# Low parts of seven output-projection weight blocks: a negated high part plus an accumulating DMA in place of a vector subtraction

## The chip, the cores and the metric

The kernel runs on one core of a Trainium2 chip. The metric is device time in microseconds (us) of one execution; three timed runs of the kernel before gave 924.5, 924.59 and 924.91 us (median 924.59). All positions below are us from the start of the profiled span.

## The reference

One decoder layer on a 1024 x 1024 residual stream in float32: RMS norm, an input projection, two head groups (a pooling mixer and a gated linear recurrence), an output projection, a squared-ReLU MLP, a gated embedding and a final norm. The line that matters here is the output projection:

```python
h = h + jnp.concatenate([y_pool, y_lru], axis=-1) @ w_out[l]
z = rms_norm(h, norm_mlp_g[l])
h = h + jnp.square(jax.nn.relu(z @ w_up[l])) @ w_down[l]
```

`w_out` is 1024 x 1024 float32.

## The kernel before

Every product of float32 matrices is made of three matmuls in the type float32r, which keeps fewer bits than float32. Each operand is split into a high part (`hi`, the value rounded to float32r) and a low part (`lo`, what the rounding lost), and `mm` (L341 to L350) issues for each block of 128 input rows `hi*hi`, then `hi` of the weights with `lo` of the data, then `lo` of the weights with `hi` of the data. All these matmuls carry line L350.

A weight block is 128 partitions x 1024 columns (512 KB). It is fetched by `load_weights` (L191): a DMA issued by SP (L196) into a tile `wo<o>_raw`, then `split` (L174): ScalarE (ACT) copies it to `wo<o>_hi` (L178), and VectorE (DVE) subtracts, `wo<o>_lo = raw - hi` (L179). Tiles `raw`, `hi` and `lo` come from pools with two buffers each, so block o+2 cannot be split before the matmuls have read block o, and its raw tile cannot be loaded before the split of an earlier block has read the raw tile whose place it takes.

The output projection has eight blocks o = 0 to 7. Each gives 8 x 3 x 2 = 48 matmuls (eight row blocks k, three products, two halves of 512 columns) into PSUM tiles `ps_o<o>`. Data are `B[0..7]`, the tiles `y0` to `y23`. Blocks 0 and 1 are interleaved (L683 to L697): k = 0 to 5 of block 0, k = 0 to 5 of block 1, k = 6, 7 of block 0, k = 6, 7 of block 1; blocks 2 to 7 follow one after another. After each block DVE adds the result to the residual stream `h` (L701), ACT squares and scales it for the next norm (L386, L389, L706), and after every second block DVE and ACT prepare operands `a` of the MLP.

Weights are asked for in the order of the list `todo` (L316 on), one block ahead. Behind `wo0` to `wo7` come the MLP weights `wu0_0`, `wu0_1`, and so on, which use the same three pools. For the first MLP pair (`up_step` with m = 0) POOL (GpSimd) makes three sums of the raw tiles (`gp`, L215), which ACT and DVE then split. A scheduler orders the instructions of each engine from the program's dependencies; each engine then runs its own list in order, and an instruction that waits holds up all behind it on that engine.

Of the kernel before, what the change touches and what calls it, by code (L numbers as in the profile page):

```python
# [10 lines left out]
AF = mybir.ActivationFunctionType  # L11
ALU = mybir.AluOpType

P = 128
S = 1024
# [6 lines left out]
URGENT = 200  # L22
# [8 lines left out]
NT = D // P  # L31
# [27 lines left out]
def block_kernel(  # L59
# [16 lines left out]
    nc = tc.nc  # L76
# [69 lines left out]
    def f32(ap):  # L146
        return ap.bitcast(F32)
# [22 lines left out]
    def pin(ins):  # L170
        return tc.keep_in_program_order(ins) if in_order else ins
# [3 lines left out]
    def split(src, hi, lo, g=None, eng=None):  # L175

        if g is None:
            first = pin(nc.scalar.activation(hi, src, AF.Copy))  # L178
            lowest[:] = [pin((eng or nc.vector).tensor_tensor(lo, src, f32(hi), ALU.subtract)).ins]  # L179
        else:  # L180
            first = pin(nc.scalar.activation(hi, src, AF.Identity, scale=g))  # L181
            lowest[:] = [pin(nc.vector.scalar_tensor_tensor(lo, src, g, f32(hi), ALU.mult, ALU.subtract)).ins]  # L182
        return first.ins

    def raw_tile(name):
        return wp.tile([P, S], F32, tag="raw", name=f"{name}_raw")

    def weight_tiles(name):
        return [wp.tile([P, S], F32R, tag=f"w{x}", name=f"{name}_{x}") for x in ("hi", "lo")]

    newest = []  # L191

    def load_weights(src, name, width=S, eng=None, queue=nc.sync, offset=0):
# [4 lines left out]
            newest[:] = [split(raw, hi, lo, eng=eng)]  # L198
        return hi, lo

    def split_weights(name, *srcs):

        hi, lo = weight_tiles(name)
        n = 0
        for src in srcs:
            w = src.shape[-1]
            split(src, hi[:, n : n + w], lo[:, n : n + w])
            n += w
        return [(hi[:, hs], lo[:, hs]) for hs in HALVES]
# [26 lines left out]
    def up_step(m, step):  # L236
        name = f"wu{m}_{step}"
        if m == 0:
            if step == 0:
                load_up(0)  # L240
            a, b, a11, a12, a21, a22 = up_blocks(0)
            s1, s2 = (R[:, hs] for hs in HALVES)
            if step == 0:
                gp(ALU.add, s1, a21, a22)
                gp(ALU.subtract, s2, s1, a11)
                gp(ALU.subtract, a21, a11, a21)
                return split_weights(name, s2, a21)
            if step == 1:
                w = split_weights(name, a22, s1)
                load_up(1)  # L250
                return w
            if step == 2:
                w = split_weights(name, a11, a12)
                up_lower[0, 3] = lowest[0]
                dv(ALU.subtract, a12, a12, s2)
                return w
            return split_weights(name, a12)
# [37 lines left out]
    def down_step(c, kind, q):  # L295
# [22 lines left out]
    todo = [  # L318
        (load_weights, w_lru[k * P : (k + 1) * P, :], f"wl{k}", 3 * P)
        for k in range(1, NT)  # L320
    ]
    todo += [(load_weights, w_in[i], f"wi{i}", S, None, nc.sync, URGENT * (i > 2)) for i in range(9)]
    todo += [(load_weights, w_out[o], f"wo{o}", S, None, nc.sync, URGENT * (o == 0)) for o in range(NT)]
    todo += [(up_step, m, step) for m in range(NPAIR) for step in range(4)]
    todo += [(down_step, c, kind, q) for c, kind in KINDS for q in range(NQ)]
    for g, os in enumerate(FETCH):
# [154 lines left out]
    for k in range(NT):  # L481
# [3 lines left out]
        for hs in halves:  # L485
            nc.sync.dma_start(H[k][:, hs], xT[k * P : (k + 1) * P, hs])  # L486
            if k == hs.start == 0:
                raw = raw_tile("wl0")[:, : 3 * P]
# [659 lines left out]
    for g, hs in enumerate(GROUPS):  # L1148
# [5 lines left out]
        for n, o in enumerate(ORDER[g]):  # L1154
# [18 lines left out]
            if g == 0 and 1 <= n < 5:  # L1173
                raw = wp.tile([P, S], F32, tag="raw", name=f"wg0_{n + 3}_raw")
# [100 lines left out]
```

## Time and profile before

| what | value |
|---|---|
| median of three timed runs | 924.59 us |
| the profiled execution's own time | 924.56 us |
| its span, first to last instruction | 922.8 us |
| outside the span | 1.76 us |
| TensorE (PE) busy | 914.6 us, 99% |
| DVE busy | 760.6 us, 82% |
| ACT busy | 459.1 us, 50% |
| POOL busy | 5.8 us, 1% |
| granted TensorE clock, mean | 0.999 |
| DMA moved | 123.97 MB, 134 GB/s |

Rows of groups read: line, engine, operation, out<-in, count, then durations in ns (min/median/max) and first and last start. Rows of a timeline read: start, duration, engine, line, operation, out<-in, count, and in brackets how long the engine idled before it and what ended that. A matmul of 128x512 is shown with 379 ns, but matmuls are pipelined: one starts about 0.216 us after the other. SP's and POOL's DMA issues are given with the time from issue to landing.

### The profile page before, as it was taken

The numbers are of one execution on the slowest core, as the hardware profiler recorded it, in microseconds if no ns is written. First come the engines' busy times: TensorE is split into PE (matmuls) and PEld (weight loads), VectorE is DVE, ScalarE is ACT, GpSimd is POOL, SyncE is SP. The second block draws the span as 40 slices with busy tenths as digits, with TensorE's granted clock in tenths as the row PEclk, the third lists the DMA queues.
The fourth block names the chain that finished last, engine by engine and source line by source line (L and its number), as shares of the span: only waits on it lengthen the run. The fifth ranks groups of instructions, "written<-read, shape, count | busy, mean of one in ns | idle before, by whom it ended". The sixth has DMA issues, their size and how long they took to land.

```text
span 922.8 us, 11209 instructions
## 1 busy us (share of the span) xinstructions
PE 914.6 (99%) x4357; PEld 798.6 (87%) x4357; DVE 760.6 (82%) x915; ACT 459.1 (50%) x535; POOL 5.8 (1%) x7
## 2 busy tenths in 40 slices
PE   9999999999999999999999999999999999999997
PEld 7888888888888888888888888888888888888896
DVE  6997984669998888888888989979786669885676
ACT  7567892447543343334334654443444347652545
POOL 0000000002000000000000000000000000000000
PEclk9999999999999999999999999999999999999999
DMA  7210143112154345344534989366632341031022
GB/s 267 90 56 27 43 167 108 69 45 69 70 189 164 126 169 198 136 141 171 191 125 148 340 315 345 109 198 205 197 114 92 114 160 45 2 136 46 1 92 92
DMA packets 45044, 123.97 MB, mean 134 GB/s; under 512 B 4160, under 2 KB 6208, under 8 KB 44992
## 3 DMA queue, kind: packets, MB, share of 16 engines
q1 hardware_dynamic: 44848, 123.22, 38.2%
q8 instruction: 34, 0.56, 0.2%
q14 instruction: 18, 0.15, 0.1%
q10 hardware_dynamic: 144, 0.04, 0.0%
HBM read 89.69 MB, written 33.55 MB: 134 GB/s over the span
## 4 chain that ended last, share of the span: by engine, by line
PE 98%; DMA 1%; DVE 0%; SPq 0%; ACT 0%; issue 0%; DVEq 0%
PE ps_P_u L350 31%; PE ps_P_d L350 31%; PE ps_i L350 10%; PE ps_e L350 10%; PE ps_o L350 9%; PE ps_l L350 3%; PE ps_j L350 1%; PE ps_g L564 1%; DMA h<-in_xT 1%; PE ps_p L350 1%; PE n_ps L417 0%; PE n_ps L416 0%; DVE t L1123 0%; SPq L486 0%; DVE a L182 0%; ACT a L181 0%
## 5 line engine op out<-in xcount | busy, mean ns | idle before, releaser
L350 PE MATMUL ps_P_d<-a,wd_P_hi 128*128 128x512 f32 x880 | 261.7, 379 | 0.0
L350 PEld LDWEIGHTS ps_P_d<-a,wd_P_hi 128*128 128x128 f32 x880 | 166.3, 189 | 23.6
L350 PE MATMUL ps_P_d<-a,wd_P_lo 128*128 128x512 f32 x440 | 166.8, 379 | 0.0
L350 PE MATMUL ps_P_u<-a,wu_hi 128*128 128x512 f32 x512 | 152.3, 379 | 0.0
L350 PE MATMUL ps_P_u<-y,wu_hi 128*128 128x512 f32 x384 | 114.2, 379 | 0.0
L350 PEld LDWEIGHTS ps_P_u<-a,wu_hi 128*128 128x128 f32 x512 | 96.8, 189 | 13.8
L350 PE MATMUL ps_P_u<-a,wu_lo 128*128 128x512 f32 x256 | 97.0, 379 | 0.0
L350 PEld LDWEIGHTS ps_P_d<-a,wd_P_lo 128*128 128x128 f32 x440 | 83.2, 189 | 11.8
L350 PEld LDWEIGHTS ps_P_u<-y,wu_hi 128*128 128x128 f32 x384 | 72.6, 189 | 10.3
L740 DVE TENSOR_TENSOR t<-t,ps_P_u 128x512 f32<-128x512 f32 (+1 forms) x80 | 62.6, 782 | 20.4 <-PE ps_P_u L350 20.4
L350 PE MATMUL ps_i<-a,wi_hi 128*128 128x512 f32 x288 | 74.3, 380 | 0.0
L350 PE MATMUL ps_P_u<-y,wu_lo 128*128 128x512 f32 x192 | 72.8, 379 | 0.0
L178 ACT ACTIVATE a<-wd 128x1024 fp32r<-128x1024 f32 x56 | 59.0, 1055 | 22.2 <-DMA wd<-act 13.8
L179 DVE TENSOR_TENSOR a<-wd,a 128x1024 fp32r<-128x1024 f32 x56 | 67.2, 1220 | 1.2 <-ACT a L178 0.8
L350 PE MATMUL ps_o<-y,wo_hi 128*128 128x512 f32 x256 | 65.7, 379 | 0.0
L350 PEld LDWEIGHTS ps_i<-a,wi_hi 128*128 128x128 f32 x288 | 54.1, 189 | 8.9 <-issue 1.0
L178 ACT ACTIVATE wu_hi<-wu 128x1024 fp32r<-128x1024 f32 x24 | 25.4, 1059 | 69.8 <-PE ps_P_u L350 44.1
L178 ACT ACTIVATE wu_hi<-wu_raw 128x1024 fp32r<-128x1024 f32 (+1 forms) x26 | 25.3, 976 | 66.3 <-PE ps_P_u L350 41.3
L350 PEld LDWEIGHTS ps_o<-y,wo_hi 128*128 128x128 f32 x256 | 48.4, 189 | 6.8
L350 PEld LDWEIGHTS ps_P_u<-a,wu_lo 128*128 128x128 f32 x256 | 48.4, 189 | 6.8
L178 ACT ACTIVATE wd_P_hi<-wd 128x1024 fp32r<-128x1024 f32 x24 | 25.3, 1055 | 46.4 <-PE ps_P_d L350 46.4
L389 ACT ACTIVATE t<-h 128x512 f32<-128x512 f32 (+2 forms) x44 | 32.0, 732 | 29.0 <-DVE h L1041 21.0
(236 smaller groups left out, 1507.6 us busy)
## 6 DMA issues: line engine op xcount, KB each, us to landing
wd<-act SPq DMA_DIRECT2D x56, 512.0 KB, 5.8
act<-t SPq DMA_DIRECT2D x32, 512.0 KB, 4.4
wu_raw<-in_w_up SPq DMA_DIRECT2D x16, 512.0 KB, 3.3
wu<-in_w_up SPq DMA_DIRECT2D x16, 512.0 KB, 4.0
act<-wu SPq DMA_DIRECT2D x16, 512.0 KB, 4.7
wd<-in_w_down SPq DMA_DIRECT2D x16, 512.0 KB, 6.7
h<-in_xT SPq DMA_DIRECT2D x14, 512.0 KB, 4.4
wg_raw<-in_w_gate SPq DMA_DIRECT2D x10, 512.0 KB, 3.2
```

What stands on the lines that cost most here:

```text
L178: first = pin(nc.scalar.activation(hi, src, AF.Copy))
L179: lowest[:] = [pin((eng or nc.vector).tensor_tensor(lo, src, f32(hi), ALU.subtract)).ins]
L350: ins = nc.tensor.matmul(ps, w, turns(z[:, hs]), start=first and z is zhi and w is whi, stop=last and w is wlo, skip_group_check=more,)
L389: pin(nc.scalar.activation(sq, t[:, hs], AF.Square))
L564: nc.tensor.matmul(x, w[r, o * P : (o + 1) * P], turns(z[r, at : at + HALF]), start=n == 0, stop=n == 2)
L740: (eng or nc.vector).tensor_tensor(to, to if y is None else y, x, ALU.add)
```

## The change

For blocks 1 to 7 the low part is made without DVE. ACT writes the high part as before, then ACT writes `-hi` into the low tile, and a DMA issued by POOL adds the raw weights to the low tile in memory (`accum_op=ALU.add`), so that the tile ends as `raw - hi`. The source of that DMA is the array in DRAM for odd blocks, and the raw tile on chip for even blocks. Block 0 is split as before. `newest` keeps its meaning; `lowest` is not set by the new function.

```diff
+    def load_added(src, name, far):
+        raw = raw_tile(name)
+        hi, lo = weight_tiles(name)
+        nc.sync.dma_start(raw, src)
+        first = pin(nc.scalar.activation(hi, raw, AF.Copy))
+        pin(nc.scalar.activation(lo, f32(hi), AF.Copy, scale=-1.0))
+        nc.gpsimd.dma_start(lo, src if far else raw, accum_op=ALU.add)
+        newest[:] = [first.ins]
+        return hi, lo
...
-    todo += [(load_weights, w_out[o], f"wo{o}", S, None, nc.sync, URGENT * (o == 0)) for o in range(NT)]
+    todo += [(load_added, w_out[o], f"wo{o}", o % 2) if o else (load_weights, w_out[o], f"wo{o}", S, None, nc.sync, URGENT) for o in range(NT)]
```

The ten new lines shift all later lines: L350 becomes L360, L386 and L706 become L396 and L716. Seven DVE subtractions go, seven ACT instructions and seven POOL DMAs come. The order of instructions moves at three places.

On TensorE, where block 2 begins (block numbers stand in the names: `ps_o2` is its result, `wo2_hi` and `wo2_lo` its weights), the kernel before runs:

```order
L350 MATMUL ps_o2_1344<-y0_113,wo2_hi_1307 128x512 x2
L350 MATMUL ps_o2_1344<-y1_114,wo2_hi_1307 128x512 x2
L350 MATMUL ps_o2_1344<-y0_113,wo2_lo_1308 128x512 x2
L350 MATMUL ps_o2_1344<-y2_115,wo2_hi_1307 128x512 x2
L350 MATMUL ps_o2_1344<-y3_116,wo2_hi_1307 128x512 x2
```

and the changed kernel at the same place:

```order
L360 MATMUL ps_o2_1347<-y0_113,wo2_hi_1308 128x512 x2
L360 MATMUL ps_o2_1347<-y1_114,wo2_hi_1308 128x512 x2
L360 MATMUL ps_o3_0_1408<-y0_113,wo3_hi_1341 128x512
L360 MATMUL ps_o3_512_1409<-y0_113,wo3_hi_1341 128x512
L360 MATMUL ps_o3_0_1408<-y1_114,wo3_hi_1341 128x512
L360 MATMUL ps_o2_1347<-y0_113,wo2_lo_1309 128x512 x2
L360 MATMUL ps_o2_1347<-y2_115,wo2_hi_1308 128x512 x2
```

Three matmuls of block 3, which need `wo3_hi`, now stand ahead of the first matmul that reads `wo2_lo`; the rest of TensorE's order is unchanged.

On ACT, from the split of block 1 on, the kernel before has (`t<-h` are the squares and scalings of the residual stream, `y22` the last operand of block 0 and 1, `a` operands of the MLP):

```order
L178 ACTIVATE wo1_hi_1210<-wo1_raw_1209 128x1024
L603 ACTIVATE t_68<-t_68 128x1024
L178 ACTIVATE y22_130<-t_68 128x1024
L178 ACTIVATE wo2_hi_1307<-wo2_raw_1306 128x1024
L386 ACTIVATE t_68<-h_67 128x1024
L706 ACTIVATE t_68<-h_67,vecs_137 128x1024
L178 ACTIVATE wo3_hi_1339<-wo3_raw_1338 128x1024
L389 ACTIVATE t_68<-h_67 128x1024
```

and the changed kernel:

```order
L205 ACTIVATE wo1_hi_1210<-wo1_raw_1209 128x1024
L206 ACTIVATE wo1_lo_1211<-wo1_hi_1210 128x1024
L613 ACTIVATE t_68<-t_68 128x1024
L178 ACTIVATE y22_130<-t_68 128x1024
L205 ACTIVATE wo2_hi_1308<-wo2_raw_1307 128x1024
L206 ACTIVATE wo2_lo_1309<-wo2_hi_1308 128x1024
L396 ACTIVATE t_68<-h_67 128x1024
L716 ACTIVATE t_68<-h_67,vecs_137 128x1024
L205 ACTIVATE wo3_hi_1341<-wo3_raw_1340 128x1024
L399 ACTIVATE t_68<-h_67 128x1024
L716 ACTIVATE t_68<-h_67,vecs_137 128x1024
L206 ACTIVATE wo3_lo_1342<-wo3_hi_1341 128x1024
```

Each negation follows its high part at once, except for block 3, where two instructions on the residual stream stand between; `wo3_hi` has one more instruction ahead of it. For blocks 4 to 7 the pair stands together as for block 2.

[...]

```order
L207 DMA wo1_lo_1211<-in_w_out 128x1024
L207 DMA wo2_lo_1309<-wo2_raw_1307 128x1024
L207 DMA wo3_lo_1342<-in_w_out 128x1024
L207 DMA wo4_lo_1403<-wo4_raw_1401 128x1024
L207 DMA wo5_lo_1474<-in_w_out 128x1024
L207 DMA wo6_lo_1535<-wo6_raw_1533 128x1024
L207 DMA wo7_lo_1606<-in_w_out 128x1024
L225 ISA
L225 TENSOR_TENSOR rstd_71<-wu0_1_raw_1666 128x512
L225 TENSOR_TENSOR rstd_71<-rstd_71,wu0_0_raw_1665 128x512
L225 TENSOR_TENSOR wu0_1_raw_1666<-wu0_0_raw_1665,wu0_1_raw_1666 128x512
```

Before, the `ISA` row stood first in the program, with nothing to wait for; now it stands behind seven DMAs, each of which waits for ACT's negation of its block.

On SP the order of loads is unchanged, but what they wait for differs: the raw tile of an odd block is given up by ACT's high part instead of DVE's subtraction, and the raw tile of an even block by the landing of its accumulating DMA.

## The prediction

> **What bounds the kernel now.** First the page's busy shares and the chain of waits, then the waits of TensorE, then a window table over the stage that is changed.
>
> ```profile
> PE 914.6 (99%) x4357; PEld 798.6 (87%) x4357; DVE 760.6 (82%) x915; ACT 459.1 (50%) x535; POOL 5.8 (1%) x7
> 143.46 82.88 PE ps_o L350 x384
> PE ps_l L480 <- DVE heat L367: 1.1, 1, 1.1
> PE n_ps L1102 <- DVE t L1101: 0.6, 1, 0.6
> 143.30:226.18 82.88, 82.88 (x386) 72.58 (x384) 51.67 (x59) 38.39 (x43) 5.56 (x3) 1.00 0.17 59
> ```
>
> TensorE (PE) is the bound. The chain runs through the output projection as one piece of 384 matmuls, 0.216 us each, and the window from 143.30 to 226.18 shows PE busy for all of its 82.88 us. The two waits of PE lie at the very start and the very end of the program. So in this stage nothing can be gained: DVE may be relieved of anything, and the end does not move. What can move it is a tile that comes too late for its matmul. The question is how late the low parts get.
>
> **What goes.** Seven subtractions, of 1.22 us:
>
> ```profile
> L179 DVE TENSOR_TENSOR wo_lo<-wo_raw,wo_hi x8: 1215/1218/1226, 139.8 to 206.6; 128x1024 fp32r<-128x1024 f32 x8
> ```
>
> They free 7 x 1.22 = 8.5 us of DVE, which lie beside PE's work and are worth nothing by the chain.
>
> **What comes.** Per block one more ACT instruction, taken as long as the high part's (1.05 us, rows below), and then a DMA of 512 KB that reads the raw weights and the low tile and writes the low tile. ACT has room (38.39 us busy of 82.88). What counts is the latency L from the end of the negation to a low tile that PE may use. No row of before shows such a DMA, so I bound it by DMAs of the same size.
>
> ```profile
> wo_raw<-in_w_out SPq DMA_DIRECT2D x8, 512.0 KB, 3.2
> out<-h SPq DMA_DIRECT2D x2, 1024.0 KB, 4.2
> out<-h SPq DMA_DIRECT2D x2, 512.0 KB, 3.0
> DMA to landing us min/median/max: 3.1/3.2/4.2
> DMA to landing us min/median/max: 3.2/5.2/10.6
> 211.65 2.18 POOL L215 TENSOR_TENSOR rstd<-wu_raw 128x512 f32<-128x512 f32 x1 [211.21 <-DMA wu_raw<-in_w_up]
> 216.01 1.28 POOL L215 TENSOR_TENSOR wu_raw<-wu_raw,wu_raw 128x512 f32<-128x512 f32 x1
> ```
>
> Below: 3.1 us, the fastest plain load of a `wo_raw` tile (first of the two landing rows). Above: 10.6 us, the slowest 512 KB load of `w_down` weights, in the busiest stage (second row). Nothing excludes a value between. I take 3.2 for the plain load, 1.2 for reading the same bytes a second time (1024 KB against 512 KB to `out`: 4.2 less 3.0), and 1.5 for POOL to issue it (POOL's shortest and longest instructions on a tile of half this size take 1.28 and 2.18): **L = 5.9 us**. [...]
>
> **Where the allowances are.** Block 1 first.
>
> ```profile
> 144.30 1.04 ACT L178 ACTIVATE wo_hi<-wo_raw 128x1024 fp32r<-128x1024 f32 x1
> 151.93 0.59 PE L350 MATMUL ps_o<-y,wo_lo 128*128 128x512 f32 x2
> 143.30:151.07 7.77, 7.77 (x38) 6.80 (x36) 5.52 (x7) 4.12 (x4) 0.00 (x0) 1.00 0.50 163
> ```
>
> `wo1_hi` ends at 145.34, the negation at 146.4, and the first matmul with `wo1_lo` starts at 151.93. A late tile also lays bare its weight load, 0.2 us, so the allowance is 5.3 us. In this window the DMA engines are half busy (share 0.50) with loads of `h` and of the next raw weights, so I give this DMA one more transfer of 512 KB: 5.9 + 1.2 = 7.1. **Wait at block 1: 7.1 - 5.3 = 1.8 us.** Everything behind moves with it, so the next places are counted in before's times.
>
> Block 2 is the tight one, since its buffers are those of block 0, which PE reads until just before it needs block 2.
>
> ```profile
> 161.25 1.06 ACT L178 ACTIVATE wo_hi<-wo_raw 128x1024 fp32r<-128x1024 f32 x1 [10.95 <-PE ps_o L350]
> 162.89 1.06 ACT L386 ACTIVATE t<-h 128x1024 f32<-128x1024 f32 x1 [0.58 <-DVE h L701]
> 163.85 1.14 ACT L706 ACTIVATE t<-h,vecs 128x1024 f32<-128x1024 f32 x1
> 164.89 1.04 ACT L178 ACTIVATE wo_hi<-wo_raw 128x1024 fp32r<-128x1024 f32 x1
> 164.02 1.03 PE L350 MATMUL ps_o<-y,wo_hi 128*128 128x512 f32 x4
> 164.88 0.59 PE L350 MATMUL ps_o<-y,wo_lo 128*128 128x512 f32 x2
> ```
>
> `wo2_hi` ends at 162.31, the negation at 163.4. PE starts block 2 at 164.02 and wants `wo2_lo` at 164.88. The scheduler has put three matmuls of block 3 in front, and those want `wo3_hi`. On ACT `wo3_hi` stands behind the negation and the two instructions on `h`: 163.4, 164.45, 165.5, so it ends at 166.5. PE waits 164.88 to 166.5 (1.6 us) for it, runs the three until 167.15, and then waits for `wo2_lo`, which comes at 163.4 + L = 169.3. Without waits PE would be through the three at 165.53. The wait is the greater of 1.6 and 163.4 + L - 165.53 + 0.2 = L - 1.9. **Wait at block 2: 5.9 - 1.9 = 4.0 us.**
>
> Block 3: its negation has two more ACT instructions ahead and ends at 169.5, its tile comes at 169.5 + L; PE reaches it a whole block after `wo2_lo`, at about 173 + L. Hidden for any L. Blocks 4 to 7:
>
> ```profile
> 174.20 1.06 ACT L178 ACTIVATE wo_hi<-wo_raw 128x1024 fp32r<-128x1024 f32 x1 [2.62 <-issue]
> 205.23 1.06 ACT L178 ACTIVATE wo_hi<-wo_raw 128x1024 fp32r<-128x1024 f32 x1 [6.51 <-PE ps_o L350]
> ```
>
> PE ends block 2 at 174.40 before; the high part stands 0.2 us ahead of that, the negation ends 2.0 behind it. PE then has block 3 to do, 45 matmuls or 9.7 us, and four of block 4 (0.86). The allowance is 9.7 + 0.86 - 0.2 - 2.0 = 8.4 us at block 4, and 9.0 at blocks 5 to 7 (48 matmuls). At 5.9 the DMA is covered by these matmuls. If that cover went, each us of L above 8.4 (then 9.0) would cost a us per block.
>
> SP's queue: raw tiles of even blocks are now held until their DMA lands, some 5 us longer; the load of block 5 that waits for block 2's lands near 173 and is used at 184.5, so it is hidden too. ACT's seven negations and what stands behind them (squares and scalings of `h`) have the same cover as DVE's subtractions had.
>
> **What stands behind the DMAs on POOL** is the reload of POOL's library (`ISA`) and the three sums for the first MLP weights.
>
> ```profile
> 216.08 0.63 ACT L178 ACTIVATE wu_hi<-rstd 128x512 fp32r<-128x512 f32 x1 [3.70 <-POOL rstd L215]
> 217.32 0.63 ACT L178 ACTIVATE wu_hi<-wu_raw 128x512 fp32r<-128x512 f32 x1 [0.61 <-POOL wu_raw L215]
> 221.29 6.05 DVE L182 SCALAR_TENSOR_TENSOR y<-h,vecs,y 128x512 fp32r<-128x512 f32 x9
> 227.26 1.28 DVE L701 TENSOR_TENSOR h<-h,ps_o 128x512 f32<-128x512 f32 x2
> 232.74 2.36 DVE L179 TENSOR_TENSOR a<-t,a 128x1024 fp32r<-128x1024 f32 x2 [0.53 <-ACT a L178]
> 123.72 1.28 ACT L592 ACT_TABLE_LOAD   x1
> ```
>
> ACT waits for these sums, and behind them stand the splits of `y`, the last addition to `h` and the last operands `a`, the first of which ends at 233.95, when PE wants it at 234.17. So a POOL that is late by x delays PE by x less 0.2. POOL is through its seventh DMA at 205.23 + 2.2 + 1.5 = 208.9 and began the sums at 211.65, so the reload may take 2.7 us unseen; the raw tile it needs even lands 1.6 us sooner, being freed by ACT. The nearest row for a reload is ACT's table load, 1.28 us. The reload's end of range below is nothing, above no row bounds it (211 us of idle covered it before). I take 1.28, hidden by POOL's wait for that raw tile.
>
> **Sum.** 1.8 + 4.0 = 5.8 us on the profiled execution's 924.56 (span 922.8 and 1.76 around it; the median of the timed runs is 924.59): **930.4 us**. With both ends of L: at 3.1, block 2 waits 1.6 for `wo3_hi` and nothing else: 926.2. At 10.6: 5.3 (without a further allowance for other traffic) + 8.7 + 2.2 + 3 x 1.6 = 21: 945.6.
>
> **The rivals.**
>
> [...]
>
> (C) A long DMA with a clock that falls.
>
> ```profile
> 1.05 4.02 PE L480 MATMUL ps_l<-heat 128*128 128x512 bf16 x9 [1.05 <-DVE heat L367]
> 4.63 1.54 PE L350 MATMUL ps_l<-a,wl_hi 128*128 128x512 f32 x4
> ```
>
> After the idle start nine matmuls take 3.58 us (1.05 to 4.63), 0.40 each against 0.216, which is 1.6 us lost. If L is 8, the waits are 3.9 + 6.1, the second long enough to be such an idle start: 10 + 1.6 = 11.6, or 936.2. [...] Against it: the slow landings are from stages with far more traffic.
>
> (D) Not slower. If the DMA lands as fast as a plain load (L up to 3.7), it is hidden at block 1, and at block 2 PE waits only for `wo3_hi`: 1.6 us, 926.2, which is within 0.2%. It decides at L = 3.7. For it: eight loads of `wo_raw` at 3.1 to 4.2. Against: the DMA reads twice as much and is issued by an engine that issued none. That the change does nothing at all is excluded as a gain, since DVE was not waited for.
>
> **How the numbers follow.** Forecast 45%, B 28%, C with all longer L 16%, D 9%, something else 2%. The range runs from D's and the lower bound's 926.2 to 939, past B and the middle of C, and leaves out the long end of C (about 8%) and some of what I have not thought of. A measurement of this kernel tells about 0.2% (1.9 us) from no change, so slower by more than that holds the forecast, B and C: 0.90; within it D: 0.09; faster 0.01.
>
> **What would show it.** In the changed profile: PE's waits, now empty in this stage, should list a wait of about 1.8 us ahead of the first `ps_o` matmul with `wo1_lo` and about 4.0 us in two pieces ahead of `ps_o2`, the first ended by ACT's `wo_hi`, the second by the DMA; none at blocks 3 to 7. The issues on POOL's line L207 should show about 6 us to landing (less POOL's own 1.5). [...] C would show in matmuls of 0.4 us behind the wait. The forecast is wrong if L is under 4 or over 7.5, if the first DMA is much slower than the others, or if PE waits anywhere else.

## The result and the profile after

Four timed runs of the changed kernel gave 928.72, 931.07, 931.41 and 931.52 us (median 931.24), beside a median of 924.64 us of the kernel before: ratio 1.0065, 95% interval 1.0047 to 1.0083. The change makes the kernel 6.6 us slower. The profiled execution is the shortest of the four: span 926.9 us, 4.1 us longer than before's 922.8.

TensorE (PE) is still the bound. This is the first row of the page, and then the list of PE's waits:

```profile
PE 915.8 (99%) x4357; PEld 797.8 (86%) x4357; DVE 754.5 (81%) x908; ACT 465.6 (50%) x542; POOL 11.3 (1%) x14
```

```profile
PE ps_o L360 <- ACT wo_hi L205: 1.3, 1, 1.3
PE ps_o L360 <- DMA wo_lo<-wo_raw: 1.2, 1, 1.2
PE ps_l L490 <- DVE heat L377: 1.1, 1, 1.1
PE n_ps L1112 <- DVE t L1111: 0.6, 1, 0.6
```

The last two were there before. The first two are new, and both stand at block 2. The page's busy share does not tell them: it is 99% in both kernels.

Block 1 in the timeline (start, duration, engine, line, operation):

```profile
145.45 1.06 ACT L206 ACTIVATE wo_lo<-wo_hi 128x1024 fp32r<-128x1024 f32 x1
146.82 1.03 POOL L207 DMA_DIRECT2D wo_lo<-in_w_out  x1 [146.37 <-ACT wo_lo L206]
151.17 1.03 PE L360 MATMUL ps_o<-y,wo_hi 128*128 128x512 f32 x4
152.23 0.70 PE L360 MATMUL ps_o<-y,wo_lo 128*128 128x512 f32 x2
```

The four matmuls from 151.17 on are through at 152.03 (0.216 us each), and the first one with `wo1_lo` starts at 152.23: a wait of 0.2 us, too short for the list. From the end of the negation (146.51) to that matmul are 5.7 us.

Block 2 and the start of block 3:

```profile
162.69 1.06 ACT L206 ACTIVATE wo_lo<-wo_hi 128x1024 fp32r<-128x1024 f32 x1
165.64 1.04 ACT L205 ACTIVATE wo_hi<-wo_raw 128x1024 fp32r<-128x1024 f32 x1
164.06 0.87 POOL L207 DMA_DIRECT2D wo_lo<-wo_raw  x1 [16.21 <-ACT wo_lo L206]
164.42 1.03 PE L360 MATMUL ps_o<-y,wo_hi 128*128 128x512 f32 x4
166.73 0.92 PE L360 MATMUL ps_o<-y,wo_hi 128*128 128x512 f32 x3 [1.28 <-ACT wo_hi L205]
168.89 0.70 PE L360 MATMUL ps_o<-y,wo_lo 128*128 128x512 f32 x2 [1.25 <-DMA wo_lo<-wo_raw]
```

PE is through four matmuls at 165.28, stands until `wo3_hi` comes, does the three matmuls that were moved ahead until 167.48 (0.32 + 0.216 + 0.216; the first behind a wait takes 0.1 longer), stands again until `wo2_lo` comes, and goes on at 168.89: 1.45 + 1.41 = 2.9 us. The low tile comes 5.1 us after the negation's end (163.75). In the windows (columns: PE busy, PEld, DVE, ACT, POOL, granted clock, DMA share, GB/s) this is, but for the 0.2 us at block 1, the only stretch of the projection in which PE is not busy throughout; all of blocks 3 to 7 lie in the second row, without a gap:

```profile
164.42:169.43 5.01, 2.48 (x11) 1.54 (x10) 3.74 (x6) 5.01 (x6) 0.51 (x1) 1.00 0.82 195
169.43:229.64 60.21, 60.21 (x280) 52.73 (x279) 35.51 (x40) 31.90 (x37) 9.24 (x8) 1.00 0.38 89
```

The DMAs on line L207 (duration of POOL's issue, min/median/max in ns; then us from issue to landing):

```profile
L207 POOL DMA_DIRECT2D wo_lo<-in_w_out x4: 865/865/1026, 146.8 to 211.1; - x4
L207 POOL DMA_DIRECT2D wo_lo<-wo_raw x3: 867/867/870, 164.1 to 200.8; - x3
DMA to landing us min/median/max: 4.5/5.1/5.5
```

And the end of POOL's list, with what DVE does beside it:

```profile
211.13 0.86 POOL L207 DMA_DIRECT2D wo_lo<-in_w_out  x1 [9.49 <-ACT wo_lo L206]
213.19 1.59 POOL L225 TENSOR_TENSOR rstd<-wu_raw 128x512 f32<-128x512 f32 x1 [1.19 <-DVE t L400]
212.96 4.07 DVE L721 TENSOR_TENSOR t<-t 128x512 f32<-128x512 f32 x3
```

POOL idles 1.2 us between its last DMA and its first sum, and the `ISA` row lies in that time. That this row reloads POOL's library is my reading of the program; the traces show no such row, only that it takes no longer than those 1.2 us. Against PE's own position (shifted by 3.5 us) the sums start earlier than before, not later.

So the profiled execution lost 0.1 us ahead of the stage, 0.2 at block 1, 2.9 at block 2, 0.3 in the first matmuls behind these three waits and 0.6 in the MLP, half of that in its first half. The half in the MLP's second half is a wait of PE near 557.9 for a low tile that DVE makes (`wd_P_lo`): 0.3 us here, 0.6 in the profile of block 2 only and 1.0 in that of the plain copy below, and none in the changed kernel's second profile; what makes it come and go was not tried. Open were two things: why three of four runs took some 2.5 us more, and what the 0.3 in the first half is.

### The profile page after: what moved, and what is told of

It is laid out like the page before. It is cut to its first block, busy times and chain, and to the rows that moved or that the text cites. A ratio compares the mean times of both kernels' runs of the same rounds, so it can differ in the third digit from the quotient of the medians.

```text
span 926.9 us, 11237 instructions
## 1 busy us (share of the span) xinstructions
PE 915.8 (99%) x4357; PEld 797.8 (86%) x4357; DVE 754.5 (81%) x908; ACT 465.6 (50%) x542; POOL 11.3 (1%) x14
## 4 chain that ended last, share of the span: by engine, by line
PE 86%; issue 5%; DMA 4%; DVE 3%; ACT 2%; SPq 0%; POOL 0%; DVEq 0%; POOLq 0%
PE ps_P_u L360 30%; PE ps_P_d L360 27%; PE ps_e L360 10%; PE ps_i L360 7%; PE ps_o L360 7%; PE ps_l L360 3%; PE ps_j L360 1%; DMA t<-in_w_down 1%; DMA act<-t 1%; DMA wd<-act 1%; PE ps_g L574 1%; DMA h<-in_xT 1%; DMA wo_lo<-wo_raw 1%; DVE wd_P_lo L179 0%; DVE t L222 0%
## 5 line engine op out<-in xcount | busy, mean ns | idle before, releaser
L360 PE MATMUL ps_P_d<-a,wd_P_hi 128*128 128x512 f32 x880 | 261.7, 379 | 0.0
L360 PEld LDWEIGHTS ps_P_d<-a,wd_P_hi 128*128 128x128 f32 x880 | 166.3, 189 | 23.6
L360 PE MATMUL ps_P_d<-a,wd_P_lo 128*128 128x512 f32 x440 | 166.9, 379 | 0.1
L360 PE MATMUL ps_P_u<-a,wu_hi 128*128 128x512 f32 x512 | 152.6, 379 | 0.0
L360 PE MATMUL ps_P_u<-y,wu_hi 128*128 128x512 f32 x384 | 114.2, 379 | 0.0
L360 PEld LDWEIGHTS ps_P_u<-a,wu_hi 128*128 128x128 f32 x512 | 96.8, 189 | 14.1 <-DVE a L179 0.4
L360 PE MATMUL ps_P_u<-a,wu_lo 128*128 128x512 f32 x256 | 97.0, 379 | 0.0
L360 PEld LDWEIGHTS ps_P_d<-a,wd_P_lo 128*128 128x128 f32 x440 | 83.2, 189 | 12.2 <-DVE wd_P_lo L179 0.5
L360 PEld LDWEIGHTS ps_P_u<-y,wu_hi 128*128 128x128 f32 x384 | 72.6, 189 | 10.3
L360 PE MATMUL ps_i<-a,wi_hi 128*128 128x512 f32 x288 | 74.3, 380 | 0.0
L360 PE MATMUL ps_P_u<-y,wu_lo 128*128 128x512 f32 x192 | 72.8, 379 | 0.0
L360 PE MATMUL ps_o<-y,wo_hi 128*128 128x512 f32 x256 | 66.0, 379 | 1.3 <-ACT wo_hi L205 1.3
L360 PEld LDWEIGHTS ps_i<-a,wi_hi 128*128 128x128 f32 x288 | 54.1, 189 | 8.9 <-issue 1.0
L360 PEld LDWEIGHTS ps_o<-y,wo_hi 128*128 128x128 f32 x256 | 48.3, 189 | 8.5 <-ACT wo_hi L205 1.7
L360 PEld LDWEIGHTS ps_P_u<-a,wu_lo 128*128 128x128 f32 x256 | 48.4, 189 | 6.9
L400 DVE TENSOR_TENSOR t<-t 128x512 f32<-128x512 f32 (+2 forms) x44 | 36.1, 820 | 15.3 <-ACT t L399 15.1
```

What stands on the lines that cost most here:

```text
L360: ins = nc.tensor.matmul(ps, w, turns(z[:, hs]), start=first and z is zhi and w is whi, stop=last and w is wlo, skip_group_check=more,)
L400: self.eng.tensor_tensor(self.acc[:, hs], self.acc[:, hs], sq, ALU.add)
```

## Experiments

My theory: all that matters is PE's wait for the low tiles of blocks 1 and 2, and the landing of block 1's DMA differs from execution to execution. The rival: POOL's reload behind the seven DMAs differs, and its sums come late. The table gives the median of each kernel, its ratio to the kernel before on the same chip with the 95% interval, and from its profiled execution the length of the projection (first `ps_o` to first `ps_P_u` matmul) and of the MLP's first half (first `ps_P_u` matmul to the first of `ps_P_d`), in us. The kernel before was timed again beside each series: 924.87 beside "changed, again" to "block 2 only", 924.49 beside "all from the raw tile" to "block 2 only, plain copy", 925.10 beside the last three.

| kernel | median | ratio | projection | MLP, first half |
|---|---|---|---|---|
| before | 924.64 | 1 | 82.9 | 291.0 |
| changed | 931.24 | 1.0065 [1.0047, 1.0083] | 86.2 | 291.3 |
| changed, again | 930.05 | 1.0059 [1.0044, 1.0073] | 87.7 | 291.3 |
| blocks 3 to 7 only | 925.16 | 1.0005 [0.9996, 1.0013] | 82.9 | 291.3 |
| sums on DVE | 930.13 | 1.0060 [1.0046, 1.0073] | 91.9 | 291.0 |
| block 2 only | 928.21 | 1.0035 [1.0023, 1.0047] | 85.8 | 291.0 |
| all from the raw tile | 930.71 | 1.0066 [1.0054, 1.0079] | 85.7 | 294.0 |
| block 1 only | 926.73 | 1.0024 [1.0013, 1.0035] | 84.8 | 291.0 |
| block 2 only, from DRAM | 929.41 | 1.0056 [1.0043, 1.0070] | 86.6 | 291.0 |
| block 2 only, plain copy | 926.18 | 1.0017 [1.0009, 1.0026] | 84.5 | 291.0 |
| two DMAs at blocks 4 to 6 | 930.42 | 1.0060 [1.0046, 1.0073] | 87.2 | 291.3 |
| two DMAs at block 2 | 931.52 | 1.0068 [1.0056, 1.0081] | 89.9 | 291.0 |
| block 1 from the raw tile | 929.29 | 1.0043 [1.0030, 1.0055] | 87.6 | 291.4 |

### The changed kernel once more

No edit.

> The changed kernel once more, nothing edited. Its profiled execution lost 4.1 us of span: 0.4 by block 1, 3.1 at block 2, and about 0.6 behind the projection, where POOL's sums are late; but three of its four timed runs lasted 931.1 to 931.5, 2.5 us longer than the profiled one of 928.72. Theory 1: PE's waits for the accumulating DMA at blocks 1 and 2 are what varies (the landing is longer in some executions). A profile of a long execution then shows these two waits adding up to about 6 us, landings on POOL's line over 5 us for the first two, and the same tail. Theory 2: what varies is the library reload on POOL behind its seven DMAs. A profile of a long execution then shows 3.5 us up to the end of the projection, POOL's first sum about 2.5 us later than 213.2, and PE waiting those 2.5 us at ps_P_u. Both: median 928.5 to 931.5.

Six runs: 928.32 to 933.53, median 930.05. The profiled one lasted 930.02. Its list of PE's waits, and the landing of block 1's DMA alone:

```profile
PE ps_o L360 <- DMA wo_lo<-in_w_out: 1.5, 1, 1.5
PE ps_o L360 <- ACT wo_hi L205: 1.3, 1, 1.3
PE ps_o L360 <- DMA wo_lo<-wo_raw: 1.2, 1, 1.2
```

```profile
DMA to landing us min/median/max: 6.8/6.8/6.8
```

The wait at block 1 is now on the list, because the landing took 6.8 us instead of 5.4; block 2 and the MLP's first half are as in the first profile. That is theory 1, in an execution of middling length; the longest, 933.53, was not profiled.

### Accumulating DMA for blocks 3 to 7 only

```diff
-    todo += [(load_added, w_out[o], f"wo{o}", o % 2) if o else (load_weights, ..., URGENT) for o in range(NT)]
+    todo += [(load_added, w_out[o], f"wo{o}", o % 2) if o > 2 else (load_weights, ..., URGENT * (o == 0)) for o in range(NT)]
```

> The accumulating DMA only for blocks 3 to 7; blocks 1 and 2 are subtracted on DVE as before. Theory 1 (all the loss that matters is PE waiting for the low tiles of blocks 1 and 2): no wait of PE in the projection, tail as in the changed kernel at most (+0.6): 924.6 to 925.3, and runs close together. Theory 2 (the reload on POOL, still behind five DMAs, gives 2.5 us in most executions): 925.2 in some runs and 927.7 in most. If a block between 3 and 7 is not hidden after all, the trace shows a wait of PE ended by a DMA there and the time lies above 925.3.

925.16 us, within 0.2% of the kernel before, though five subtractions are gone from DVE. The list of PE's waits has only the two rows of before:

```profile
PE ps_l L490 <- DVE heat L377: 1.1, 1, 1.1
PE n_ps L1112 <- DVE t L1111: 0.6, 1, 0.6
```

Blocks 3 to 7 are hidden, the reload behind their DMAs lies in the 1.2 us for which POOL waits for `wu_raw` and costs nothing that can be measured, and the relief of DVE is worth nothing. The MLP's first half has the 0.3 us too.

### The sums on DVE instead of POOL

```diff
     def gp(op, to, x, y):
-        return nc.gpsimd.tensor_tensor(to, x, y, op).ins
+        return nc.vector.tensor_tensor(to, x, y, op).ins
```

> The changed kernel with the three sums for the MLP weights on DVE instead of POOL, so that POOL runs no arithmetic and reloads no library. Theory 1: the waits at blocks 1 and 2 stay (3.5 us in the profile, more in other executions); the three sums cost DVE 2 to 4 us in a stage where it has slack: 928 to 931, runs as far apart as those of the changed kernel. Theory 2: no reload, so all runs agree at 924.6 + 3.5 = 928.1, less than 0.5 us apart.

Median 930.13, from 928.6 to 933.51: as slow and as spread as the changed kernel, though POOL has no sum left to reload a library for. The rival falls. The profiled execution happens to be the longest, and shows what a long one is made of. PE at block 1:

```profile
150.92 1.03 PE L360 MATMUL ps_o<-y,wo_hi 128*128 128x512 f32 x4
154.29 0.70 PE L360 MATMUL ps_o<-y,wo_lo 128*128 128x512 f32 x2 [2.35 <-DMA wo_lo<-in_w_out]
154.83 1.18 PE L360 MATMUL ps_o<-y,wo_hi 128*128 128x512 f32 x4
155.81 1.06 PE L360 MATMUL ps_o<-y,wo_lo 128*128 128x512 f32 x2
156.66 1.91 PE L360 MATMUL ps_o<-y,wo_hi 128*128 128x512 f32 x4
```

The landing took 7.7 us, so PE stood from 151.78 to 154.29, 2.5 us. Then the matmuls come 0.43 us apart instead of 0.216 (two at 155.81 take 0.85, four at 156.66 take 1.71). The windows show the clock (columns as above, the clock is third from the end):

```profile
155.00:159.11 4.11, 4.11 (x13) 3.28 (x13) 0.00 (x0) 0.00 (x0) 0.00 (x0) 0.58 0.02 5
172.63:177.00 4.37, 4.37 (x13) 3.61 (x14) 3.85 (x6) 2.73 (x3) 0.86 (x1) 0.61 0.88 236
```

A granted clock of 0.58 for 4.11 us is 4.11 x 0.42 = 1.7 us lost, and it happens again behind the wait at block 2 (4.37 x 0.39 = 1.7). With 2.5 and 2.8 us of waits and 0.2 in the first matmuls behind them that is 8.9; the projection is 9.0 longer than before's 82.9.

### Block 2 alone

```diff
-    ... f"wo{o}", o % 2) if o else ...
+    ... f"wo{o}", o % 2) if o == 2 else ...
```

> The accumulating DMA only for block 2 (source: the raw tile on chip). The three matmuls of block 3 stay ahead of the first one with wo2_lo, and POOL's reload has 45 us of cover. Theory 1: PE waits for wo3_hi and then for the DMA, together what the changed kernel showed there less the 0.4 by which it was already shifted, so 3.1 to 3.5 us: 927.7 to 928.1 where the landing is 4.5 us, and as much more as the landing is longer in an execution. Theory 2: 927.7 to 928.1 in all runs. My prediction's own figure for this block was 4.0: 928.6.

928.21, 3.3 us above its kernel before. PE's waits:

```profile
PE ps_o L360 <- ACT wo_hi L178: 1.3, 1, 1.3
PE ps_o L360 <- DMA wo_lo<-wo_raw: 1.1, 1, 1.1
```

The landing was 4.6 us, the projection 2.9 us longer. One block makes over half of the loss. Its runs still lie 2.2 us apart (927.19 to 929.42), so block 1 is not all that varies.

### All sources on chip

```diff
-    ... f"wo{o}", o % 2) if o else ...
+    ... f"wo{o}", 0) if o else ...
```

> The changed kernel with the raw tile on chip as the source of all seven accumulating DMAs, the array in DRAM for none. In the profiles of the changed kernel the wait at block 1 was 0.3, 1.5 and 2.4 us with landings of 5.5, 6.8 and 7.7 us, while the on-chip source landed in 4.5 every time. Theory 1 (the DRAM source is what is slow and varies): landing about 4.6 at block 1, low tile 5.2 behind the negation, allowance 5.3, no wait there; block 2 as in the kernel with block 2 alone; 928.2 to 928.6, runs about 2 us apart. Theory 2 (it is the place, with other traffic, or the first DMA of the queue): block 1 still waits 0.3 to 2.4 and the time stays at 929 to 933.

Both theories missed the time: 930.71. The projection does what theory 1 said (block 1 landed in 4.9, no wait there, 85.7 us), but the MLP's first half is 3.0 us longer. PE's waits and then SP's and POOL's rows:

```profile
PE ps_P_u L360 <- DVE wu_lo L179: 1.6, 1, 1.6
PE ps_P_u L360 <- DVE a L179: 0.8, 1, 0.8
```

```profile
204.96 11.61 SPq L240 DMA_DIRECT2D wu_raw<-in_w_up  x2
219.50 1.27 POOL L225 TENSOR_TENSOR rstd<-wu_raw 128x512 f32<-128x512 f32 x1 [7.92 <-DMA wu_raw<-in_w_up]
```

The raw tile of block 7 is now held until its DMA has landed (issued at 210.7, landed 5.5 later), and the second load of MLP weights must wait for that tile. It lands near 219.5, POOL's sums start 6.3 us later than at 213.19, and what ACT and DVE do behind them is late. In the changed kernel block 7 reads DRAM, so ACT's high part gives its raw tile up.

### Block 1 alone, and block 2 alone from DRAM

```diff
-    ... f"wo{o}", o % 2) if o else ...
+    ... f"wo{o}", o % 2) if o == 1 else ...        (block 1 only)
+    ... f"wo{o}", 1) if o == 2 else ...            (block 2 only, from DRAM)
```

> The accumulating DMA only for block 1, source DRAM, as in the changed kernel; all other blocks on DVE. Theory 1: waits of 0.3 to 2.4 us at block 1, nothing at block 2, no late sums on POOL: 925.2 to 927.3, and up to 1.7 more in an execution in which the clock falls behind the wait; median about 926.2. My prediction's figure for this block was 1.8: 926.7. If the waits of blocks 1 and 2 do not simply add, this and the kernel with block 2 alone (928.21) do not sum to the changed kernel's 930.05.

926.73, 2.2 us above before (925.2 to 928.36). In the profiled execution the DMA landed in 7.0 us and PE waited for it:

```profile
PE ps_o L360 <- DMA wo_lo<-in_w_out: 1.6, 1, 1.6
```

Blocks 1 and 2 alone cost 2.2 and 3.3; together 5.5, against the changed kernel's 5.2 (second series) and 6.6 (first). They add, as far as runs that lie 2 to 5 us apart can tell.

> The accumulating DMA only for block 2, with the array in DRAM as its source; all else as in the kernel with block 2 alone from the raw tile (928.21, landing 4.6). Theory 1 (the DRAM source is slow and varies): landing 5.3 to 7.7, 929 to 931.5, median about 930, runs further apart than with the near source. Theory 2 (block 1's place made it vary): landing 5.3 in every run, 928.9, runs as close as with the near source.

929.41, 1.6 us more above before than with the on-chip source (4.9 against 3.3). The landing in the profile is 5.4 against 4.6; runs lie 1.8 us apart, no further than from on chip. So the DRAM source is about 0.7 us slower here. The other 0.9 of the medians fits a fall of the clock: the three longest runs list a mean clock of 0.995 to 0.996, the two shortest 0.997 and 0.998. Over all profiles the landings from DRAM were 5.4, 6.8, 7.0 and 7.7 us at block 1 and 5.1 to 5.9 elsewhere, but for one of 7.6 at block 5; from on chip 4.5 to 5.0, but for the 5.5 above. All the long ones read DRAM, and most of them at block 1. The traces show one thing more that they share: in the 8 us from POOL's issue, SP's queue moved 948 to 1024 KB beside each of the four long ones, that is two loads of 512 KB, and at most 512 KB beside 18 of the 20 others from DRAM. The remaining two (block 1 of the first profile, and block 2 here) had 948 and 964 KB beside them and landed in 5.4. So two loads alongside go with the long landings but do not always make one. With next to nothing beside them (0 to 48 KB), three landings from DRAM took 5.3 to 5.4, where those from on chip took 4.5 to 4.6 (again but for that 5.5), so the source alone makes about 0.8. The kernels that read block 1 from on chip do not part source and loads: the next load then waits for the raw tile, and in the first 5 us SP moved some 220 to 240 KB instead of 480 to 530. No kernel here kept the DRAM source and moved the loads away.

### A copy in place of the addition

```diff
-        nc.gpsimd.dma_start(lo, src if far else raw, accum_op=ALU.add)
+        nc.gpsimd.dma_start(lo, src if far else raw)
```

and block 2 only, as above.

> As the kernel with block 2 alone from the raw tile, but the DMA copies instead of adding, so that the low tile of block 2 holds the raw weights (the low product of this block is left wrong). It prices the read of the destination, which my prediction took at 1.2 us. If it costs that: landing 3.4 instead of 4.6, PE waits 1.3 for the high part of block 3 and about 0.5 for the low tile: 927.0. If the add costs nothing: landing 4.6 and 928.2. If nearly all of the landing is the add: landing under 3 and 926.4, where the wait for the high part of block 3 alone stays.

926.18. The low tile of block 2 now holds the raw weights instead of `raw - hi`. The landing and POOL's issue:

```profile
DMA to landing us min/median/max: 3.0/3.0/3.0
```

```profile
163.35 0.69 POOL L207 DMA_DIRECT2D wo_lo<-wo_raw  x1 [162.90 <-ACT wo_lo L206]
```

The addition costs 1.6 us of the 4.6 (and 0.3 of POOL's issue, which lies inside the landing time). With 3.0 the low tile is there when PE wants it, and only the wait for `wo3_hi` is left.

### Two DMAs one behind the other

```diff
-        pin(nc.scalar.activation(lo, f32(hi), AF.Copy, scale=-1.0))
-        nc.gpsimd.dma_start(lo, src if far else raw, accum_op=ALU.add)
+        pin(nc.scalar.activation(lo, f32(hi), AF.Copy, scale=-float(times)))
+        [nc.gpsimd.dma_start(lo, src if far else raw, accum_op=ALU.add) for _ in range(times)]
```

with `times` = 2 for blocks 4 to 6 (3 and 7 have one) in the first kernel, and for block 2 alone in the second.

> The kernel with accumulating DMAs for blocks 3 to 7 only (925.16), but blocks 4, 5 and 6 get two of them, one behind the other, over a low tile that ACT filled with minus twice the high part; the low part of these three blocks comes out doubled, left so. It doubles the suspected cost where I said it is covered by 8.4 us (block 4) and 9.0 (5, 6). Two landings of 4.5 from the raw tile and the steps around them make about 9.9 us from negation to use (two from DRAM 11.2 or more). Theory 1 (the cover is as worked out, and a wait at one block lengthens the cover of the next): waits of 1.5 at block 4, 0.8 at block 5, none at 6: 927.4. Theory 2 (each block pays alone, as the prediction put it): 1.5 + 2.2 + 0.9: 929.7. Theory 3 (the cover is much larger, or both DMAs run side by side): 925.2.

930.42, above all three. The trace shows why:

```profile
187.55 0.87 POOL L207 DMA_DIRECT2D wo_lo<-in_w_out  x1 [4.64 <-ACT wo_lo L206]
195.40 0.87 POOL L207 DMA_DIRECT2D wo_lo<-in_w_out  x1 [6.98 <-DMA wo_lo<-in_w_out]
186.64 0.70 PE L360 MATMUL ps_o<-y,wo_lo 128*128 128x512 f32 x2 [0.27 <-DMA wo_lo<-wo_raw]
200.74 0.70 PE L360 MATMUL ps_o<-y,wo_lo 128*128 128x512 f32 x2 [3.47 <-DMA wo_lo<-in_w_out]
```

Block 4 had its tile 9.7 us after the negation and PE waited 0.4, so the cover is 9.3 (worked out: 9.0 with 48 matmuls of block 3, as here). At block 5 the first DMA took 7.6 to land, the tile came 13.4 after the negation, and PE waited 3.6: a cover of 9.8, which is block 4's plus the 0.4 of its wait. Block 6 waited for nothing, its cover lengthened by those 3.6. The way the waits are linked is theory 1's; the DRAM landing was longer than I had put in.

> The kernel with the accumulating DMA for block 2 alone (928.21), but two of them, one behind the other, over a low tile filled with minus twice the high part; the low part of block 2 comes out doubled, left so. Theory 1 (every us of landing at block 2 is a us of PE): 1.3 us wait for the high part of block 3, then about 6 us for the low tile, 4.8 more than with one: 933.0 without a fall of the clock. The wait of 6 us is over twice the 2.4 behind which the matmuls fell to 0.42 us apiece, so the clock falls in every run and adds 1.7: 934.7. Theory 2 (the two run side by side): 929 to 930.

931.52, 6.4 above before, less than theory 1 said. The scheduler had answered: with the later tile it placed seventeen matmuls of block 3 ahead instead of three.

```profile
166.53 1.13 PE L360 MATMUL ps_o<-y,wo_hi 128*128 128x512 f32 x4 [1.33 <-ACT wo_hi L178]
173.90 1.10 PE L360 MATMUL ps_o<-y,wo_lo 128*128 128x512 f32 x2 [3.03 <-DMA wo_lo<-wo_raw]
```

```profile
173.90:178.30 4.40, 4.40 (x13) 3.57 (x14) 0.00 (x0) 0.00 (x0) 0.00 (x0) 0.61 0.35 119
```

The second wait is 3.2 us instead of 6 (the row's 3.03 counts from the end of a matmul shown with 0.38), and the clock falls behind it, 4.40 x 0.39 = 1.7 us.

### The changed kernel with block 1 from the raw tile

```diff
-    ... f"wo{o}", o % 2) if o else ...
+    ... f"wo{o}", o % 2 * (o > 1)) if o else ...
```

> The changed kernel (930.05 to 931.24) with one source exchanged: the DMA of block 1 reads the raw tile on chip instead of the array in DRAM; blocks 3, 5 and 7 keep DRAM. With all sources on chip the wait at block 1 was gone, but the raw tile of block 7 was given up late, POOL's sums started 6 us later and PE lost 3 us in the MLP. Theory: here only the first happens: no wait at block 1, 3.1 at block 2, 0.3 in the tail: 928.2 to 928.6, runs 2 us apart. If the variation of the changed kernel does not come from block 1's DRAM read, the median stays at 930 to 931.

929.29, or 4.2 above before instead of 5.2 to 6.6. The wait at block 1 is gone (landing 4.9), and the MLP has the 0.3 and no more. It is 0.7 above my expectation, and the profiled execution has a fall of the clock at block 2, behind the same two waits (1.3 and 1.2) that the changed kernel's profile shows without a fall:

```profile
168.03:171.60 3.57, 3.56 (x9) 2.90 (x10) 3.05 (x6) 2.74 (x3) 0.87 (x1) 0.52 0.80 248
```

3.57 x 0.48 = 1.7 us. Why the same waits bring a fall here and none there can be read from the traces. In all thirteen profiles the granted clock, between its first rise and the end of the program, changes only after whole multiples of 3.41 us: each fall lasts 3.41, and the two in the kernel with the sums on DVE are 13.65 (4 x 3.41) apart; from the first rise to the fall at the end it is 914.77 us in the kernel before and 918.19 in the changed kernel's first profile, 268 and 269 times 3.413. Cut along these steps, first this kernel and then the changed kernel's first profile show:

```profile
164.63:168.04 3.41, 0.92 (x4) 0.49 (x4) 2.14 (x4) 3.41 (x5) 0.00 (x0) 1.00 1.05 221
168.04:171.46 3.42, 3.42 (x8) 2.79 (x9) 2.90 (x4) 2.73 (x3) 0.87 (x1) 0.50 0.84 259
164.53:167.94 3.41, 1.83 (x8) 0.95 (x6) 2.14 (x4) 3.41 (x5) 0.40 (x1) 1.00 0.87 154
167.94:171.36 3.42, 2.47 (x11) 2.19 (x12) 2.90 (x5) 2.91 (x4) 0.86 (x1) 1.00 0.80 298
```

Here both waits lie in one step, PE is busy for 0.92 of its 3.41 us, and the next step runs at half the clock. In the changed kernel's profile a border falls between the waits, each step keeps PE busy for longer, and no fall follows. Between 100 and 900 us of all thirteen profiles the four steps with PE busy for 1.28 us or less were each followed by a fall, and of the others, with 1.48 or more, none was. So in these profiles a fall went with how much of one step PE stood idle (2.1 us by this count were followed by one, 1.9 were not), and the borders lie at different places of the program: 0.2 us behind the start of the first wait here (164.44), 0.75 ahead of it (165.28) in the changed kernel's first profile.

That some of the runs of block 2 alone are 2 us longer than others fits this, though their long executions were not profiled: the two longest list a mean clock of 0.995 and 0.996, the others 0.997 to 0.998. One run does not fit: 929.45 of the kernel of this section lists 0.999, like its shortest of 927.74.

## Why the prediction was right, and where its terms were off

The forecast was 930.4 by waits of PE at blocks 1 and 2 for the low tile; measured were 931.24 and 930.05. The mechanism is the one foreseen, and blocks 1 and 2 alone add up to it. That the sum comes so close is in part luck: block 2 and its L were taken too long, and falls of the clock and waits in the MLP, which the sum put at nothing, filled the difference. By the prediction's own signs it came near to failing: one landing at block 1 made L 8.0, over its limit of 7.5, and PE waited at two places in the MLP. The terms:

- **PE bound, DVE's relief worth nothing.** Right: with five of seven blocks changed the time stays within 0.2% of before.
- **L = 3.2 + 1.2 + 1.5 = 5.9.** Too long by 0.8 at block 2 (5.1). POOL's issue is 0.87 to 1.03 us and is no term of its own: it lies inside the 4.5 to 5.0 from issue to landing. A plain copy takes 3.0, the addition 1.6 more; 0.3 passes from the negation to the issue.
- **Block 2: 4.0 us.** Measured 2.9 (3.1 with the slower first matmuls), in the two pieces and with the two releasers named. The difference is L's.
- **Block 1: L = 7.1, a wait of 1.8.** In four profiles L was 5.7, 7.2, 7.3 and 8.0, the wait 0.2, 1.7, 1.8 and 2.5. The figure is in the middle, but it was put together from a base that is too long by 0.8 and 1.2 for other traffic: from on chip the same place landed in 4.9, with fewer loads beside, from DRAM in 5.4 to 7.7. Two loads beside go with the long landings, as the 1.2 assumed, but above a landing of 5.4 they cost anything from 0 to 2.3 us; that it differs by 2 us between executions was not foreseen. The allowance of 5.3 was right to 0.2 (5.7 left a wait of 0.2).
- **Blocks 3 to 7 hidden.** Right. The allowance of 9.0 was measured as 9.3. That each us above it would cost a us per block is wrong: a wait at one block lengthens the cover of the next.
- **POOL's reload hidden.** Right, at 1.2 us or less against 1.28 taken. Rival B, a reload that is not hidden, falls: no run shows a reload longer than 1.2 us, and with no sum on POOL the time is the same (930.13 against 930.05). What I did not see is that the sums, now earlier against DVE's work, meet DVE's products (4.07 us for three instead of 1.89), which goes with 0.3 us in the MLP. With the sums on DVE, and wherever block 7 is subtracted as before, the 0.3 is gone. The other 0.3 of the first profile is the wait for `wd_P_lo`, which the second does not have; its cause stays open.
- **Rival with a falling clock.** I tied it to a landing of 8 us and a single long wait. It needs neither: it came behind an idle time of 2.5 us, and behind the two short waits at block 2 where both lay in one step of 3.41 us. Each fall costs 1.7 (I had 1.6). It is a part of the time that was missing in the forecast and made up for block 2's being too long.
- **Not slower, 926.2 if L is at most 3.7.** The price was right: the copy at block 2, with 0.3 + 3.0 = 3.3, lies 1.7 above its kernel before (926.18 against 924.49), where 1.6 was taken. The addition's 1.6 decides against it.

What stays open: the runs of 931.1 to 931.5 of the first series were not profiled. Two of them list a mean clock of 0.995, which fits a fall; the third lists 0.999, so there a long landing alone would have to be the cause. No kernel here beats the one before: PE has no gap in this stage, so a change on DVE can only keep the time or lose some.

## What to carry to other kernels

Before work is moved off an engine that nobody waits for, look for the place with the least time between the last read of a buffer and the first need of its next contents: there a longer path (a negation of 1.06 and then 5.1 us, instead of one DVE instruction of 1.2) cost 2.9 of its 5 us more, while one block later all of it is hidden. Two blocks of seven made nearly the whole loss, and a kernel that had left those two alone would have lost nothing measurable. When a transfer reads a tile that others wait to reuse, count how long it holds that tile too; it is a wait on another queue (with all sources on chip it made the MLP's first half 3.0 us longer).

## What the runs showed that I had not expected

- An accumulating DMA of 512 KB took 4.5 to 5.0 us from on chip (5.5 once), and from DRAM mostly 5.1 to 5.9, but up to 7.7 without a change in the program. One fixed duration is not enough where the allowance lies within that spread (5.3 at block 1).
- The granted clock fell to one half for 3.41 us behind single idle times of 2.5 and 3.2 us, and behind two of 1.4 us with three matmuls between them, but the latter not every time: in these profiles it came where 2.1 us or more of the idle time lay within one step of 3.41 us, not where 1.9 or less did, and the borders of these steps lay 0.2 us behind the start of the first wait in one execution and 0.75 ahead of it in another.
- POOL's sums and DVE's products of two tiles took longer when they ran side by side: 1.59 to 1.73 and 1.36 us apiece in the changed kernel's first profile. A sum with DVE idle beside it took 1.28 (the second one with all sources on chip), and with the sums on DVE, three of DVE's products take 0.63 apiece:

```profile
218.37 1.89 DVE L721 TENSOR_TENSOR t<-t 128x512 f32<-128x512 f32 x3
```

  In the 4.07 us of DVE's three products POOL ended two sums and began the third; one after the other, at 0.63 and 1.28 apiece, three and two would take 4.5. Why the two are slower side by side was not shown.
